# Chunk outputs with swapped operands and TensorE transposes, and a zero fill moved to another place on ScalarE, in a two-block transformer kernel

## Chip, cores, metric

The kernel runs on one core of one Trainium2 chip. The metric is device time in microseconds (us) of one execution. A core has five engines with a program each: TensorE (PE, with its weight loads PEld), VectorE (DVE), ScalarE (ACT), GpSimd (POOL) and SyncE (SP). Each works off its own instructions in order; semaphores hold one back until what it needs is there. Sixteen DMA engines move data between DRAM and the on-chip memory; SP and ACT issue the transfers that matter here, and a row "SPq" or "ACTq" is the stretch in which an engine issues one.

## What is computed

Two blocks on a sequence of 256 tokens of width 1024 in float32. The change touches the first half of the first block only:

```
x = concat(meta_tokens[16], x[256])            # 272 positions
p = rms_norm(x) @ w_in                          # q 512, k 128, v 128, u 512
a = sliding_window_attention(q, k, v)           # 8 heads of 64, window 128, sinks, meta keys always seen
s = s5_ssm(u)                                   # 32 groups of 16 channels, 64 complex states each
    bu = u B;  state[t] = A * state[t-1] + bu[t];  y = Re(C state) + D u
    z  = gelu(y);  s = z * sigmoid(z @ glu_w + glu_b)
h = x + concat(rms_norm(a), rms_norm(s)) @ w_out
```

After it come a product-key expert layer (PEER: 16384 experts, 8 heads with 16 experts each per token, with a weighted scatter and two large matrix products) and a second block of two attention layers. They are the remaining 1200 us, and neither the code nor the order of their instructions changes.

## The kernel before

**Matrix products.** Large products split each float32 operand into a rounded part and a rest and run three matmuls (`mm3`, lines L1696 to L1698). Weights come through a feed `w` (L89, issued on SP); ACT rounds each (`H`, L102) and DVE or POOL makes the rest (`Lo`, L103).

**The SSM in chunks.** Time is cut into 34 chunks of 8 steps. `Ssm.enter` puts u through DRAM (`udr`, L552) and loads it as `U` (L556: 128 rows of step and channel, 32 groups, 34 chunks). `powers` builds maps `W` on DVE; `maps` transposes them on PE (L566) and ACT copies them to `WT` (L567). `outputs` builds tables `G` on DVE (L595 to L600, two tensors of 2304 columns). In `run`, 32 matmuls of `U` with `WT` (L639; the trace has two instructions for each) give the state inputs, which ACT copies (`s`, L644); DVE rotates, scans and rotates back to the chunk states `S` (L652 to L671). `response` multiplies `bd` and `G` on PE (L613) to the impulse response `K`, which goes to DRAM (`kdr`, L621) and comes back as the block matrix `T` (L625). A chunk output is `T` times `U` (L684) plus `G` times `S` (L691), four pairs of groups into each of four PSUM banks, taken in turn from tags y (one bank), b (two banks), y and b; ACT applies the Gelu (`zc`, L694); 16 stores and 4 loads through DRAM (`zdr`, L698; `zT`, L700) turn it to channels by time. `zT` is multiplied by the gating weights `glu` (L712), then come tanh (L736), the product `z` (L738) and the rounded `zH` (L739), the input of the SSM half of the output product.

**The attention.** The q product (L1696 to L1698 into p), its norm and transposes (L333), scores (L369), exps (L378), then for each of two token halves: transposes of the weights (L397), ACT copies (`PT`, L399), products with the values (L406, L410), `attn` (L414), norm and transposes (L423), `aH` (L424), and the attention half of the output product (`out_part`).

**What sets the order.** The attention part is written as the foreground, the SSM part as a background generator that is given room in nanoseconds by its `yield` numbers. A scheduler takes instructions in about that order, and explicit `c.after(a, b)` puts a behind b.

**The zero fill.** Expert weights are later scattered into a DRAM table `wscr` of 8 MB that must hold zeros. A tile `zero` of 128 by 256 is cleared on POOL, and four ACT-issued transfers of 2 MB each (L256) write it, behind the last `hH` turn (L233).

Of the kernel before, what the change touches and what calls it, by code (L numbers as in the profile page):

```python
# [19 lines left out]
FT = mybir.dt.float32  # L20
# [3 lines left out]
AF = mybir.ActivationFunctionType  # L24
# [149 lines left out]
SJ = 8  # L174
SC = L // SJ


def first_half(c):

    nc, tc, A = c.nc, c.tc, c.A  # L180
    V, G = nc.vector, nc.gpsimd
    f = Flow(c)
    with ExitStack() as ctx:
        one = ctx.enter_context(tc.tile_pool(name="b1", bufs=1, reuse_waits="tile"))
        pin = tc.tile_pool(name="b1in", bufs=1, side="right", reuse_waits="tile")
        inp = pin.__enter__()
# [9 lines left out]
        pk = one.tile([128, NPK1], FT, name="pk1")  # L196
        nc.sync.dma_start(pk, A["pk1"])
        c.feed.load(4)
        zero = inp.tile([128, 256], FT, name="zero")
        c.memset0 = G.memset(zero, 0.0)  # L200

        def P1(n):
            if n in PKA:
# [48 lines left out]
        ssm.enter(up)  # L252
        ssm.tables()
        ssm.outputs()
        for i in range(4):
            z = nc.scalar.dma_start(c.wscr[:, 32 * i:32 * i + 32].rearrange("p b t -> p (b t)").rearrange("p (a n) -> p a n", n=256),  # L256
                                    zero[:, None, :].to_broadcast([128, 16, 256]))
            c.after(z, c.turned)


        vr = one.tile([128, 2, 128], FT, name="vr")
# [4 lines left out]
        glu = None  # L266
# [86 lines left out]
        def attention():  # L353
# [4 lines left out]
            with tc.tile_pool(name="b1a", bufs=1, side="right", reuse_waits="tile") as work:  # L358
# [3 lines left out]
                for th in range(2):  # L362
# [19 lines left out]
                    nc.scalar.copy(Pm, S[:, :, 0:16])  # L382
                    ready.append((S, st, Pm))
                f.mark("exps")
                for th in range(2):
                    S, st, Pm = ready[th]
                    jobs = [(Pm.rearrange("p h m -> p (h m)"), None)]
                    jobs += [(S[:, h, 16 + 128 * kb:144 + 128 * kb], (h, kb)) for h in range(8) for kb in range(th + 1)]
                    o = c.psum("o")
                    prev = None  # L390
                    for j0 in list(range(0, len(jobs), 4)) + [None]:
                        nxt = None
                        if j0 is not None:
                            p = c.psum("m")
                            grp = jobs[j0:j0 + 4]
                            for n, (ap, _) in enumerate(grp):
                                nc.tensor.transpose(p[:, n * 128:(n + 1) * 128], ap, c.ident)  # L397
                            PT = work.tile([128, 512], FT, tag="PT", name="PT", bufs=2)
                            nc.scalar.copy(PT[:, :len(grp) * 128], p[:, :len(grp) * 128])  # L399
                            nxt = (grp, PT)  # L400
                            yield 109 * len(grp)
                        if prev:
                            for n, (_, hk) in enumerate(prev[0]):
                                lhs = prev[1][:, n * 128:(n + 1) * 128]
                                if hk is None:
                                    nc.tensor.matmul(o, lhs, vb.rearrange("p k r d -> p r k d"), start=True, stop=True)  # L406
                                    continue
                                h, kb = hk
                                b = 64 * (h % 2)
# [28 lines left out]
class Ssm:  # L438
# [3 lines left out]
    def __init__(self, c, one, P1):  # L442
        self.c, self.nc, self.one, self.P1 = c, c.nc, one, P1
        self.V = c.nc.vector

    def temp(self, name, i):
        return self.one.tile([128, 2304], FT, tag="t%d" % i, name=name)
# [180 lines left out]
    def run(self, glu, out):  # L628
        nc, c, V, one = self.nc, self.c, self.V, self.one
        yield 8000  # L630
        self.maps()
        yield 3000

        st = self.temp("s", 0)[:, :2 * 16 * SC].rearrange("p (z j c) -> p z j c", z=2, j=16)
        for j0, n in ((0, 6), (6, 5), (11, 5)):
            for z in range(2):
                p = c.psum("b")
                for j in range(j0, j0 + n):
                    nc.tensor.matmul(p[:, (j - j0) * 2 * SC:(j - j0 + 1) * 2 * SC], self.WT[z][:, j],  # L639
                                     self.U[:, 2 * j:2 * j + 2].rearrange("p g c -> p (g c)"), start=True, stop=True)  # L640
                v = p[:, :n * 2 * SC].rearrange("p (j g c) -> p j g c", j=n, g=2)
                for g in range(2):
                    r = slice(64 * g, 64 * g + 64)
                    nc.scalar.copy(st[r, z, j0:j0 + n], v[r, :, g])  # L644
            yield 500
        self.response()

        flat = lambda t: t.rearrange("p j c -> p (j c)")
        both = lambda z: self.R[:, None, z].to_broadcast([128, 2, 16, SC])
# [21 lines left out]
                V.tensor_tensor(S[z][r, :, g], m1[r, z, :, 1:SC - 1], m2[r, 1 - z, :, 1:SC - 1], op=(OP.subtract, OP.add)[z])  # L671
        yield 2000

        zc = self.temp("zc", 3)[:, :32 * (SC - 2)].rearrange("p (g c) -> p g c", g=32)
        self.zT = self.temp("zT", 0)[:, :4 * T].rearrange("p (a t) -> p a t", a=4)
        n = SC - 2
        dst = c.zdr.rearrange("(g p) i c -> p i g c", p=16)
        for ct in range(4):
            y = c.psum("yb"[ct % 2])
            for jj in range(4):  # L680
                j = 4 * ct + jj
                for g in range(2):
                    o = 2 * jj + g
                    m = nc.tensor.matmul(y[:, o * n:(o + 1) * n], self.T[:, 2 * j + g], self.U[:, 2 * j + g, 2:],  # L684
                                         start=(o == 0), stop=False, skip_group_check=True)
                    if o == 0:
                        first = m
                    else:
                        c.after(m, first)
                for z in range(2):  # L690
                    nc.tensor.matmul(y[:, 2 * jj * n:2 * (jj + 1) * n], self.G[z][:, j, 1:].rearrange("p a b -> p (a b)"),  # L691
                                     S[z][:, j].rearrange("p g c -> p (g c)"), start=False, stop=(z == 1), skip_group_check=True)
            gs = slice(8 * ct, 8 * ct + 8)
            nc.scalar.activation(zc[:, gs].rearrange("p g c -> p (g c)"), y[:, :8 * n], AF.Gelu)  # L694
            if ct % 2:
                h = slice(8 * ct - 8, 8 * ct + 8)
                for i in range(SJ):
                    nc.sync.dma_start(dst[:, i, h], zc[16 * i:16 * i + 16, h])  # L698
                for k in (ct - 1, ct):
                    t = nc.sync.dma_start(self.zT[:, k], c.zdr[k * 128:(k + 1) * 128].rearrange("p i c -> p (i c)"))  # L700
            yield 1500
        self.had.append(t)
        yield "exps"
        acc = [c.psum("b") for _ in range(2)]
        yield 8000

        for u, i in [(10, 0)] + [(u, 1) for u in range(11, 15)] + [(u, 2) for u in range(15, 19)]:
            if u < len(c.feed.issued):
                c.after(c.feed.issued[u], self.had[i])
        for k in range(4):  # L710
            for co in range(4):
                m = nc.tensor.matmul(acc[co // 2][:, co % 2 * T:co % 2 * T + T], glu()[:, k * 512 + co * 128:k * 512 + (co + 1) * 128], self.zT[:, k],  # L712
                                     start=(k == 0 and co % 2 == 0), stop=(k == 3), skip_group_check=True)
                if k == 0:
                    if co % 2:
                        c.after(m, first)
                    first = m
            yield 500
# [918 lines left out]
def body(tc, A, out):  # L1637
# [3 lines left out]
    with ExitStack() as ctx:  # L1641
# [79 lines left out]
        c.hscr = hscr = tc.dram_tile([128, 2, D], FT, name="hscr")  # L1721
        c.udr = tc.dram_tile([512, SJ, SC], FT, name="udr")
        c.kdr = tc.dram_tile([512, (2 * SJ - 1) * 16], FT, name="kdr")
        c.zdr = tc.dram_tile([512, SJ, SC - 2], FT, name="zdr")
        c.ascr = [tc.dram_tile([128, AB, T], FT, name="ascr%d" % i) for i in range(NB // AB)]
        c.wscr = tc.dram_tile([128, NB, 128], FT, name="wscr")
        with tc.tile_pool(name="ph", bufs=1, reuse_waits="tile") as ph:
# [51 lines left out]
def layout(inp):  # L1779
# [15 lines left out]
    A["wkv"] = chunks(w[:, 512:768])  # L1795
    A["wu"] = chunks(w[:, 768:])
    wo = g["w_out"][0]
    wo = np.concatenate([wo[:512][qp], wo[512:]], 0)
    A["wo"] = np.concatenate([chunks(wo[r:r + 512, n:n + 512]) for r in (0, 512) for n in (0, 512)], 1)
    A["glu"] = chunks(g["ssm_glu_w"][0])  # L1800

    def states(a):
        return a.reshape(16, 128).T
# [4 lines left out]
    def col(v, k):  # L1808
        return v.reshape(k, 128).T
# [4 lines left out]
    for p in range(16):  # L1814
# [6 lines left out]
          dk, col(g["ssm_glu_b"][0], 4), col(g["attn_out_g"][0][qp], 4), col(g["ssm_out_g"][0], 4),  # L1821
# [69 lines left out]
```

## Time and profile before

| | us |
|---|---|
| median of 3 runs | 1386.55 (1384.66 to 1387.51) |
| profiled execution | 1384.22, span 1382.4 |
| PE busy | 1290.8 (93%) |
| DVE, ACT, POOL busy | 931.5 (67%), 646.9 (47%), 419.9 (30%) |
| mean granted TensorE clock | 0.953 |

Times within the trace count from the start of the span. The part that the change touches ends with the first `zH` matmul, at 184.02 us; from there on the instructions of PE, DVE, ACT and SP stand in the same order before and after the change. A granted clock of 1.00 is the higher of TensorE's two levels, 0.50 the lower.

### The profile page before, as it was taken

How to read it: one execution, taken by the hardware profiler on the slowest of the kernel's cores; microseconds unless marked ns; L12 is line 12 of the kernel's file. 1: busy time of each engine (PE TensorE's matmuls, PEld its weight loads, DVE VectorE, ACT ScalarE, POOL GpSimd, SP SyncE). 2: the span in 40 equal slices, each digit the busy share in tenths (PEclk: the TensorE clock that was granted, in tenths of full speed). 3: DMA queues.
4: the chain of work that ended last, by engine and by line, in shares of the span. 5: the costliest groups of instructions: out<-in, count | busy, mean ns of one | idle time of the engine just before them, and what ended most of it. 6: DMA issues, size and time to landing. Idle time of an engine off the chain costs nothing.

```text
span 1382.4 us, 21238 instructions
## 1 busy us (share of the span) xinstructions
PE 1290.8 (93%) x7800; PEld 1121.0 (81%) x7800; DVE 931.5 (67%) x2135; ACT 646.9 (47%) x1119; POOL 419.9 (30%) x253
## 2 busy tenths in 40 slices
PE   4678999999999999998999999999998979979998
PEld 4555989999999999998777788888866768756777
DVE  6963278898898666664888855555567855585734
ACT  4324245545545444444444454444554545534552
POOL 7000000377787777700000000000033426441143
PEclk9876699999999999999999999999999999997999
DMA  5927166688887777897889866555564325551231
GB/s 198 305 36 132 24 225 209 205 218 227 228 225 212 200 204 194 241 367 241 302 300 317 298 201 193 185 191 188 187 207 140 107 95 171 202 161 53 77 107 61
DMA packets 118392, 263.80 MB, mean 191 GB/s; under 512 B 35968, under 2 KB 50176, under 8 KB 117008
## 3 DMA queue, kind: packets, MB, share of 16 engines
q1 hardware_dynamic: 80208, 228.82, 52.6%
q0 software_dynamic: 20608, 8.46, 5.2%
q10 hardware_dynamic: 17472, 25.17, 5.0%
q8 instruction: 61, 1.00, 0.3%
q14 instruction: 43, 0.35, 0.1%
HBM read 233.24 MB, written 28.90 MB: 190 GB/s over the span
## 4 chain that ended last, share of the span: by engine, by line
PE 77%; DVE 13%; DMA 6%; ACT 2%; issue 2%; SPq 0%; ACTq 0%; DVEq 0%
PE ps L884 20%; PE ps L1696 10%; PE ps L1697 10%; PE ps L1698 10%; PE pr L1696 4%; PE pr L1698 4%; PE pr L1697 4%; DMA ga<-ascr 3%; PE m L1289 2%; DVE Lo L103 2%; PE ps L1097 2%; PE o L1334 1%; DMA wscr<-zero 1%; DVE act L894 1%; PE m L369 1%
## 5 line engine op out<-in xcount | busy, mean ns | idle before, releaser
L102 ACT CAST H<-w 128x1024 fp32r<-128x1024 f32 (+1 forms) x370 | 385.9, 1045 | 513.0 <-PE ps L1697 186.1
L103 DVE TENSOR_TENSOR Lo<-w,H 128x1024 fp32r<-128x1024 f32 x310 | 387.5, 1251 | 183.3 <-ACT H L102 179.8
L103 POOL TENSOR_TENSOR Lo<-w,H 128x1024 fp32r<-128x1024 f32 (+1 forms) x60 | 142.1, 2373 | 629.1 <-ACT H L102 604.2
L1055 POOL DMA_INDIRECT wscr<-sent x128 | 241.2, 1884 | 234.2 <-DVE act L1032 169.0
L1696 PE MATMUL ps<-xH,H 128*128 128x256 f32 x1024 | 290.9, 284 | 0.0
L1697 PE MATMUL ps<-xL,H 128*128 128x256 f32 x1024 | 287.9, 281 | 0.0
L1698 PE MATMUL ps<-xH,Lo 128*128 128x256 f32 x1024 | 287.7, 281 | 0.0
L884 PE MATMUL ps<-H,a 128*128 128x512 f32 x1024 | 281.5, 397 | 5.0 <-ACT a L896 3.0
L884 PEld LDWEIGHTS ps<-H,a 128*128 128x128 f32 x1024 | 193.8, 189 | 51.0 <-ACT a L896 3.2
L1696 PEld LDWEIGHTS ps<-xH,H 128*128 128x128 f32 x1024 | 193.1, 189 | 0.0
L1698 PEld LDWEIGHTS ps<-xH,Lo 128*128 128x128 f32 x1024 | 193.1, 189 | 0.0
L1697 PEld LDWEIGHTS ps<-xL,H 128*128 128x128 f32 x1024 | 193.0, 188 | 0.0
L884 PE MATMUL ps<-Lo,a 128*128 128x512 f32 x512 | 161.5, 397 | 1.4 <-DVE Lo L103 1.3
L884 PEld LDWEIGHTS ps<-Lo,a 128*128 128x128 f32 x512 | 96.5, 189 | 25.4 <-DVE Lo L103 3.2
L894 DVE TENSOR_TENSOR act<-ga,act 128x256 f32<-128x256 f32 x128 | 47.4, 420 | 27.4 <-DMA ga<-ascr 27.3
L1696 PE MATMUL pr<-H,exH 128*128 128x512 f32 x128 | 54.7, 429 | 0.9 <-ACT exH L1137 0.9
L1696 PE MATMUL pr<-H,oxH 128*128 128x512 f32 (+1 forms) x128 | 52.8, 415 | 1.1 <-ACT oxH L1137 1.1
L897 DVE TENSOR_TENSOR a<-act,a 128x256 fp32r<-128x256 f32 x128 | 53.5, 419 | 0.0
L1697 PE MATMUL pr<-Lo,exH 128*128 128x512 f32 x128 | 52.8, 413 | 0.0
L896 ACT CAST a<-act 128x256 fp32r<-128x256 f32 x128 | 51.3, 401 | 2.9 <-DVE act L894 2.9
L1698 PE MATMUL pr<-H,exL 128*128 128x512 f32 x128 | 52.6, 411 | 0.0
L1698 PE MATMUL pr<-H,oxL 128*128 128x512 f32 (+1 forms) x128 | 52.6, 411 | 0.0
(486 smaller groups left out, 1975.1 us busy)
## 6 DMA issues: line engine op xcount, KB each, us to landing
w<-in_ut SPq DMA_DIRECT2D x128, 512.0 KB
w<-in_pv SPq DMA_DIRECT2D x128, 512.0 KB
ascr<-ga ACTq DMA_DIRECT2D x64, 256.0 KB
ga<-ascr SPq DMA_DIRECT2D x64, 256.0 KB
w<-in_we SPq DMA_DIRECT2D x32, 512.0 KB
w<-in_wod SPq DMA_DIRECT2D x28, 512.0 KB
wscr<-zero ACTq DMA_DIRECT2D x4, 2048.0 KB
w<-in_wqy SPq DMA_DIRECT2D x16, 512.0 KB
```

What stands on the lines that cost most here:

```text
L102: self.last = self.nc.scalar.copy(H, self.loaded[u])
L103: eng.tensor_sub(Lo, self.loaded[u], H.bitcast(FT))
L884: nc.tensor.matmul(acc[2 * th + n], a[:, s], b[:, n * 512:(n + 1) * 512], start=first and e == 0, stop=last and e == 2)
L894: V.tensor_tensor(src, ga[:, blk % 2], src, op=OP.mult)
L896: copied = nc.scalar.copy(aH, src)
L897: V.tensor_sub(aL, src, aH.bitcast(FT))
L1055: ins = c.nc.gpsimd.indirect_dma_start(out=c.wscr.rearrange("i b (t o) -> (i b t) o", o=1), out_offset=bass.IndirectOffsetOnAxis(ap=t.bitc ...
L1097: nc.tensor.matmul(p[:, a * 128:(a + 1) * 128], o1[:, a], o2[:, a], start=True, stop=True)
L1289: nc.tensor.matmul(sp[:, :off + nk], q(h)[:, ts], k(h)[:, :off + nk], start=True, stop=True)
L1696: nc.tensor.matmul(o, ah, bh, start=first, stop=False)
L1697: nc.tensor.matmul(o, ah, bl, start=False, stop=False)
L1698: nc.tensor.matmul(o, al, bh, start=False, stop=last)
```

## The change

1. The zero fill is issued on ACT behind the first Gelu of the chunk outputs instead of behind the last `hH` turn; its source is 128 by 128 (`self.zero`), so that each store covers 512 bytes in place of 1024.
2. `response()` comes right behind `maps()`, ahead of the state matmuls.
3. In the chunk outputs `U` (32 columns, at column position 0 or 32) and `S` (64 columns) are the stationary operands, `T` and `G` the moving ones, so that results have chunks on 64 partitions; 16 PE transposes (L704) and two DVE copies (L705) make `zT` in place of the 16 stores and 4 loads. The rows of the affected weights are permuted on the host (`cp`) to suit.
4. The transposes of the attention weights stand behind the last chunk output (`c.weighed`), a `yield` falls from 8000 to 1500, and four output weight loads no longer stand behind `zT`.

```diff
-        zero = inp.tile([128, 256], FT, name="zero")
-        c.memset0 = G.memset(zero, 0.0)
...
-        for i in range(4):
-            z = nc.scalar.dma_start(c.wscr[:, 32 * i:32 * i + 32].rearrange("p b t -> p (b t)").rearrange("p (a n) -> p a n", n=256),
-                                    zero[:, None, :].to_broadcast([128, 16, 256]))
-            c.after(z, c.turned)
...
-                                nc.tensor.transpose(p[:, n * 128:(n + 1) * 128], ap, c.ident)
+                                c.weighed.append(nc.tensor.transpose(p[:, n * 128:(n + 1) * 128], ap, c.ident))
...
         self.maps()
+        self.response()
         yield 3000
...
-        self.response()
...
-                    m = nc.tensor.matmul(y[:, o * n:(o + 1) * n], self.T[:, 2 * j + g], self.U[:, 2 * j + g, 2:],
-                                         start=(o == 0), stop=False, skip_group_check=True)
...
+                    m = nc.tensor.matmul(y[q:q + 32, o], self.U[:, 2 * j + g, 2:], self.T[:, 2 * j + g], start=(jj == 0), stop=False,
+                                         tile_position=(0, q), skip_group_check=True)
...
-                    nc.tensor.matmul(y[:, 2 * jj * n:2 * (jj + 1) * n], self.G[z][:, j, 1:].rearrange("p a b -> p (a b)"),
-                                     S[z][:, j].rearrange("p g c -> p (g c)"), start=False, stop=(z == 1), skip_group_check=True)
...
+                    m = nc.tensor.matmul(y[0:64, o], S[z][:, j].rearrange("p g c -> p (g c)"), self.G[z][:, j, 1:].rearrange("p a b -> p (a b)"),
+                                         start=False, stop=(z == 1), skip_group_check=True)
...
+            t = nc.scalar.activation(zc[0:64, h, :, j0:j0 + 4].rearrange("p i j q -> p j i q"),
+                                     y[0:64].rearrange("p (j i q) -> p j i q", j=4, i=SJ), AF.Gelu)
+            if b == 0:
+                for i in range(4):
+                    m = nc.scalar.dma_start(c.wscr[:, 32 * i:32 * i + 32].rearrange("p b t -> p (b t)").rearrange("p (a n) -> p a n", n=128),
+                                            self.zero[:, None, :].to_broadcast([128, 32, 128]))
+                    c.after(m, t)
...
-                for i in range(SJ):
-                    nc.sync.dma_start(dst[:, i, h], zc[16 * i:16 * i + 16, h])
-                for k in (ct - 1, ct):
-                    t = nc.sync.dma_start(self.zT[:, k], c.zdr[k * 128:(k + 1) * 128].rearrange("p i c -> p (i c)"))
...
+        for h in range(2):
+            p = c.psum("by"[h])
+            for i in range(SJ):
+                nc.tensor.transpose(p[:, 64 * i:64 * i + 64], zc[0:64, h, i].rearrange("p j q -> p (j q)"), c.ident[:64, :64])
+            V.tensor_copy(self.zT[:, 2 * h:2 * h + 2].rearrange("p g (i c) -> p g i c", i=SJ), p.rearrange("p (i g c) -> p g i c", i=SJ, g=2))
...
+        for m in c.weighed:
+            c.after(m, self.ylast)
```

On ACT, around the zero fill before (L233 the turn, L536 and L551 copies for the SSM, L102 the rounding of weights, L286 the first step of the k norm):

```order
L233 ACTIVATE hH<-m,pka 128x272 x2
L256 DMA wscr<-zero 128x16x256
L102 CAST H<-w 128x1024
L536 COPY bd_401<-pre 64x16x16 x2
L536 COPY bd_402<-pre 64x16x16 x2
L551 COPY uP<-p 128x34x8 x2
L551 COPY uP<-y 128x34x8
L551 COPY uP<-o 128x34x8
L256 DMA wscr<-zero 128x16x256 x3
L102 CAST H<-w 128x1024 x2
L286 ACTIVATE ks<-p 128x128
```

On ACT, around the zero fill after the change (L372 are the exps, L693 the Gelus, L394 the copies of the transposed attention weights):

```order
L372 ACTIVATE S,st<-S,st 128x272 x7
L376 COPY Pm<-S 128x128
L102 CAST H<-w 128x1024 x2
L693 ACT_TABLE_LOAD
L693 ACTIVATE zc<-y 64x4x8x16
L697 DMA wscr<-zero 128x32x128 x4
L693 ACTIVATE zc<-b 64x4x8x16
L693 ACTIVATE zc<-y 64x4x8x16
L693 ACTIVATE zc<-b 64x4x8x16
L394 COPY PT<-m 128x512 x2
L394 COPY PT<-m 128x128
```

All four transfers now stand together between the first and the second Gelu, ahead of every copy of attention weights.

On PE before, where the chunk outputs begin (L1696 to L1698 are the attention half of the output product):

```order
L1696 MATMUL p<-H,aH 128x512
L1697 MATMUL p<-Lo,aH 128x512
L1698 MATMUL p<-H,aL 128x512
L684 MATMUL y<-U,T 128x32 x2
L691 MATMUL y<-S,G_479 128x64
L691 MATMUL y<-S,G_480 128x64
L684 MATMUL y<-U,T 128x32 x2
```

On PE after the change, from the last chunk output pair to the products with the values (L392 transposes of attention weights, L704 those of `zc`, L717 the gating product, L405 products with the values):

```order
L683 MATMUL b<-T,U 32x128 x2
L689 MATMUL b<-G_478,S 64x128
L689 MATMUL b<-G_479,S 64x128
L392 MATMUL m<-cstt,Pm 128x128
L392 MATMUL m<-cstt,S 128x128 x7
L704 MATMUL b<-cstt,zc 128x64 x8
L704 MATMUL y<-cstt,zc 128x64 x8
L401 MATMUL o<-vb,PT 128x512
L405 MATMUL o<-vr,PT 128x64 x3
L392 MATMUL m<-cstt,S 128x128
L405 MATMUL o<-vr,PT 128x64 x4
L717 MATMUL b<-zT,glu 128x256 x4
```

The chunk outputs moved from inside the attention half of the output product to between scores and weighing, and the gating product from behind that half to inside the weighing.

On DVE, the tables `G` before (L103 is the rest of a weight, L287 and L1706 begin the norm of k):

```order
L595 TENSOR_TENSOR G_479<-pk_107,A 128x2304
L598 TENSOR_TENSOR G_480<-pk_107,A 128x2304
L607 MEMSET K 128x4x112
L103 TENSOR_TENSOR Lo<-w,H 128x1024 x2
L287 TENSOR_REDUCE kss<-ks 128x2 x2
L287 TENSOR_REDUCE kss<-ks 16x2
L103 TENSOR_TENSOR Lo<-w,H 128x1024
L1706 TENSOR_SCALAR rs<-kss 128x6
```

The same place after the change (L281 begins the norm of k):

```order
L592 TENSOR_TENSOR G_478<-pk_106,A 128x2304
L592 TENSOR_TENSOR tg<-pk_106,A 128x2304
L595 TENSOR_TENSOR G_479<-pk_106,A 128x2304
L594 TENSOR_TENSOR G_478<-G_478,tg 128x2304
L596 TENSOR_TENSOR tg<-pk_106,A 128x2304
L103 TENSOR_TENSOR Lo<-w,H 128x1024
L597 SCALAR_TENSOR_TENSOR G_479<-G_479,tg 128x2304
L103 TENSOR_TENSOR Lo<-w,H 128x1024
L281 TENSOR_REDUCE kss<-ks 128x2 x2
L281 TENSOR_REDUCE kss<-ks 16x2
```

The six table operations now stand nearly together; before, two stood ahead of the k norm and four were placed among its steps.

## Rows read from the trace of the kernel before

**Rows 1.** Chain that ended last, 115 to 190 us: start us, us, what

```profile
124.81 0.48 ACT PT L399
...
136.70 0.70 DVE attn L414
...
138.56 0.50 PE p L1696
...
143.63 0.36 PE y L684 x4
...
165.50 0.53 PE p L1696
...
176.21 6.06 PE b L712 x28
182.29 0.48 ACT tg L736
...
184.02 0.50 PE p L1696
```

**Rows 2.** The same view, 24 to 126 us

```profile
39.65 18.49 DMA wscr<-zero
58.16 7.69 DMA U<-udr
...
65.98 10.05 PE b L639 x46
...
86.44 1.97 PE b L639 x18
...
89.07 1.29 DVE m L652
```

**Rows 3.** Timeline of ACT, 30 to 60 us

```profile
33.78 0.39 ACTq L256 DMA_DIRECT2D wscr<-zero  x1
...
38.31 1.24 ACTq L256 DMA_DIRECT2D wscr<-zero  x1
...
39.65 12.87 ACTq L256 DMA_DIRECT2D wscr<-zero  x2
52.62 1.99 ACT L102 CAST H<-w 128x1024 fp32r<-128x1024 f32 x2 [12.21 <-issue]
```

**Rows 4.** DMA queues, 33 to 52.52 us: packets, MB, share of 16 engines

```profile
q10 hardware_dynamic: 5065, 5.15, 76.3%
```

**Rows 5.** DMA queues, 52.52 to 70 us

```profile
q10 hardware_dynamic: 3191, 3.23, 52.1%
```

**Rows 6.** Timeline of PE, 45 to 100 us

```profile
65.98 10.05 PE L639 MATMUL b<-U,WT 128*128 128x68 f32 x46 [3.88 <-DMA U<-udr]
...
89.77 2.03 PE L613 MATMUL m<-G,bd 128*32 128x128 f32 x64
```

**Rows 7.** Timeline of DVE, 36 to 95 us

```profile
51.08 2.55 DVE L595 TENSOR_TENSOR G<-pk,A 128x2304 f32<-128x2304 f32 x1
...
59.28 1.20 DVE L103 TENSOR_TENSOR Lo<-w,H 128x1024 fp32r<-128x1024 f32 x1
...
69.74 2.56 DVE L600 SCALAR_TENSOR_TENSOR G<-G,tg 128x2304 f32<-128x2304 f32 x1
```

**Rows 8.** Windows of core 0: busy us by engine, granted TensorE clock (PEclk), DMA share

```profile
66.00:76.00 10.00, 10.00 (x47) 10.00 (x48) 7.05 (x8) 2.23 (x8) 0.00 (x0) 0.50 0.01 3
86.00:88.00 2.00, 2.00 (x18) 1.91 (x18) 0.00 (x0) 0.59 (x2) 0.00 (x0) 1.00 0.00 0
```

**Rows 9.** Timeline of ACT, 118 to 190 us

```profile
142.90 1.28 ACT L694 ACT_TABLE_LOAD   x1
147.19 0.38 ACT L694 ACTIVATE zc<-y 128x256 f32<-128x256 f32 x1 [3.00 <-PE y L691]
```

**Rows 10.** DMA queues, 48 to 58 us

```profile
q10 hardware_dynamic: 3197, 3.24, 94.4%
q1 hardware_dynamic: 1758, 0.23, 15.2%
```

More of the change, by code (lines that the diff above doesn't have):

```diff
@@ L384, in attention @@
                 f.mark("exps")
+                c.weighed = []
                 for th in range(2):
@@ L444, in __init__ @@
         self.V = c.nc.vector
+        self.zero = one.tile([128, 128], FT, name="zero")
+        c.nc.gpsimd.memset(self.zero, 0.0)
     def temp(self, name, i):
@@ L644, in run @@
                     nc.scalar.copy(st[r, z, j0:j0 + n], v[r, :, g])
-            yield 500
-        self.response()
+            yield 0
         flat = lambda t: t.rearrange("p j c -> p (j c)")
@@ L672, in run @@
         yield 2000
-        zc = self.temp("zc", 3)[:, :32 * (SC - 2)].rearrange("p (g c) -> p g c", g=32)
+        zc = self.temp("zc", 3)[:, :2048].rearrange("p (h i j q) -> p h i j q", h=2, i=SJ, j=8)
         self.zT = self.temp("zT", 0)[:, :4 * T].rearrange("p (a t) -> p a t", a=4)
         n = SC - 2
-        dst = c.zdr.rearrange("(g p) i c -> p i g c", p=16)
-        for ct in range(4):
-            y = c.psum("yb"[ct % 2])
+        for b in range(4):
+            y = c.psum("yb"[b % 2])
+            prev = None
@@ L680, in run @@
             for jj in range(4):
-                j = 4 * ct + jj
+                j = 4 * b + jj
+                o = slice(128 * jj, 128 * jj + 128)
                 for g in range(2):
-                    o = 2 * jj + g
-                    m = nc.tensor.matmul(y[:, o * n:(o + 1) * n], self.T[:, 2 * j + g], self.U[:, 2 * j + g, 2:],
-                                         start=(o == 0), stop=False, skip_group_check=True)
[L686 to L689, printed above, removed]
@@ L690, in run @@
-                for z in range(2):
-                    nc.tensor.matmul(y[:, 2 * jj * n:2 * (jj + 1) * n], self.G[z][:, j, 1:].rearrange("p a b -> p (a b)"),
-                                     S[z][:, j].rearrange("p g c -> p (g c)"), start=False, stop=(z == 1), skip_group_check=True)
[L693 to L696, printed above, removed]
-                for i in range(SJ):
-                    nc.sync.dma_start(dst[:, i, h], zc[16 * i:16 * i + 16, h])
-                for k in (ct - 1, ct):
-                    t = nc.sync.dma_start(self.zT[:, k], c.zdr[k * 128:(k + 1) * 128].rearrange("p i c -> p (i c)"))
@@ L701, in run @@
-            yield 1500
-        self.had.append(t)
+                    q = 32 * g
+                    m = nc.tensor.matmul(y[q:q + 32, o], self.U[:, 2 * j + g, 2:], self.T[:, 2 * j + g], start=(jj == 0), stop=False,
+                                         tile_position=(0, q), skip_group_check=True)
+                    if prev is not None:
+                        c.after(m, prev)
+                    prev = m
+                for z in range(2):
+                    m = nc.tensor.matmul(y[0:64, o], S[z][:, j].rearrange("p g c -> p (g c)"), self.G[z][:, j, 1:].rearrange("p a b -> p (a b)"),
+                                         start=False, stop=(z == 1), skip_group_check=True)
@@ new lines, in run @@
+            self.ylast = m
+            h, j0 = b // 2, 4 * (b % 2)
+            t = nc.scalar.activation(zc[0:64, h, :, j0:j0 + 4].rearrange("p i j q -> p j i q"),
[5 more added lines that the diff above has]
+                    c.after(m, t)
@@ L703, in run @@
+            yield 500
+        for h in range(2):
[3 more added lines that the diff above has]
+            V.tensor_copy(self.zT[:, 2 * h:2 * h + 2].rearrange("p g (i c) -> p g i c", i=SJ), p.rearrange("p (i g c) -> p g i c", i=SJ, g=2))
         yield "exps"
         acc = [c.psum("b") for _ in range(2)]
-        yield 8000
-        for u, i in [(10, 0)] + [(u, 1) for u in range(11, 15)] + [(u, 2) for u in range(15, 19)]:
+        yield 1500
@@ L708, in run @@
+        for u, i in [(10, 0)] + [(u, 1) for u in range(11, 15)]:
             if u < len(c.feed.issued):
                 c.after(c.feed.issued[u], self.had[i])
+        for m in c.weighed:
+            c.after(m, self.ylast)
         for k in range(4):
@@ L1723, in body @@
         c.kdr = tc.dram_tile([512, (2 * SJ - 1) * 16], FT, name="kdr")
-        c.zdr = tc.dram_tile([512, SJ, SC - 2], FT, name="zdr")
         c.ascr = [tc.dram_tile([128, AB, T], FT, name="ascr%d" % i) for i in range(NB // AB)]
@@ L1797, in layout @@
     wo = g["w_out"][0]
-    wo = np.concatenate([wo[:512][qp], wo[512:]], 0)
+    cp = np.arange(512).reshape(2, 8, 2, 16).transpose(0, 2, 1, 3).reshape(-1)
+    wo = np.concatenate([wo[:512][qp], wo[512:][cp]], 0)
     A["wo"] = np.concatenate([chunks(wo[r:r + 512, n:n + 512]) for r in (0, 512) for n in (0, 512)], 1)
-    A["glu"] = chunks(g["ssm_glu_w"][0])
+    A["glu"] = chunks(g["ssm_glu_w"][0][cp][:, cp])
     def states(a):
@@ L1820, in layout @@
           g["ssm_c_im"][0].transpose(0, 2, 1).reshape(16, 128, 16).transpose(1, 0, 2).reshape(128, 256),
-          dk, col(g["ssm_glu_b"][0], 4), col(g["attn_out_g"][0][qp], 4), col(g["ssm_out_g"][0], 4),
+          dk, col(g["ssm_glu_b"][0][cp], 4), col(g["attn_out_g"][0][qp], 4), col(g["ssm_out_g"][0][cp], 4),
           np.tile(g["q_norm_g"][0], 2)[:, None], np.tile(g["k_norm_g"][0], 2)[:, None], rep(g["attn_sinks"][0][QPERM])]
```

## The prediction

> **What bounds the kernel now.** The kernel is one long chain that runs mostly through PE, so I read first the part of the chain of waits that the change touches. What begins with the first zH matmul at 184.02 us [rows 1] keeps its order, so the whole effect should be by how much that matmul moves. In the front, the chain runs through the zero fill and the loads of U behind it until 65.85, then through the state matmuls, the DVE chain from 89.07 on and the attention [rows 2]. At the back it is PE almost without a gap: weighing, the start of the output product at 138.56, chunk outputs from 143.63 to 165.50, the rest of the output product, the gating product to 182.27 [rows 1].
>
> The second view is the timeline of ACT around the zero fill. Four transfers of 2048 packets of 1 KB each are issued there. The first two take 0.39 and 1.24 us, the last two 12.87 us together, and the next instruction of ACT waited 12.21 us for "issue", for nothing else [rows 3]. The queue tells why: by the end of the issue, at 52.52, 5065 packets had moved [rows 4], and 3191 (a few seen in both stretches) moved afterwards [rows 5]. So ACT is let go when no more than about 3100 packets are left in its queue; until then it does nothing.
>
> **The front.** Without the fill, U's loads needn't share the DMA engines with it, and ACT isn't held from 39.65 to 52.52. This removes PE's wait of 3.88 us for U at 65.98 [rows 6]. But response() now stands ahead of the state matmuls and needs both finished tables G. DVE is packed: the first table operation starts at 51.08, behind the maps W, whose place doesn't move [rows 7]. Six of them at 2.55 us and one weight rest of 1.20 [rows 7] make 51.1 + 15.3 + 1.2 = 67.6, less a little overlap 67.5 (tables finished at 72.30 before, when nothing was in a hurry). PE then starts at 67.5 instead of 65.98. It runs the response in 2.03 us at the higher clock [rows 6], twice that at the lower, and then state matmuls. The 64 of these took 10.05 + 1.97 us before, 0.218 us each in the first stretch and 0.109 in the second [rows 2], at a granted clock of 0.50 and 1.00 [rows 8], half and full clock in the following. If the short response raises the clock earlier, up to 4 us come back. Sum: +1.5 for the start, +2.0 to +4.1 for the response (before, it lay at 89.77, under the DVE chain, and cost nothing there), +0.7 for three more q rows ahead of the last state matmul, 0 to -4 for the clock: from 0 to +6. Since q's sums are worked into the same chain later than the start of it, a part is absorbed; I take **+1.7**, with -1 to +4 as its ends. The scores keep their length, so the exps end at 124.81 + 1.7 = 126.5.
>
> **The zero fill in its new place.** It now stands on ACT behind the first Gelu. From 126.5, ACT does two casts (1.99 for two, [rows 3]), the table load (1.28, [rows 9]) and a Gelu of 64x512 (0.38 for 128x256 [rows 9], so 0.4 to 0.76): the issue starts at 130.5. There are now 4 x 4096 = 16384 packets of 512 bytes. ACT comes free when some 3100 are left, after 13284. A packet's cost: in one stretch 3197 packets of 1 KB took 94.4% of 16 engines for 10 us, 47.2 ns each, and 1758 of 131 bytes took 15.2%, 13.8 ns each [rows 10]. A line through both gives 27.9 ns at 512 bytes, over 16 engines 1.74 ns; by bytes alone it would be 23.6 (1.48 ns), by count alone 47 (2.95 ns). So 13284 packets take 23.2 us, from 19.6 to 39; I take the line, and expect small packets to be near its end. Before, packets moved at 2.95 ns each only after the first 2 to 3 us; add 1.5 to 2. That gives a release between 152 and 156, with the two weight loads that share the engines perhaps 158; I take **154.5**.
>
> Queued behind on ACT are three Gelus and all copies of attention weights (PT). The products with the values wait for PT, the transposes of zc for the Gelus, the gating product for those. PE has only the chunk outputs to do meanwhile, and the first eight transposes of attention weights. Those 128 chunk instructions now stream 128 columns. Bounds: 0.032 us each as in the response, which puts four 32-column tiles beside one another [rows 6], 0.11 to 0.22 as the state matmuls: 4 to 28 us from 121.3 on. Even 28 ends at 149, inside the hold. So swapping the operands neither gains nor costs: it is hidden, and with it the 21.9 us that the chunk outputs took before (143.63 to 165.50, [rows 1]) leave the path, to be replaced by the hold.
>
> **From the release to zH.** Three Gelus, 2.0. The rest of the transposes of zc ahead of the first value product, about 8 at 0.11 to 0.22, +1. From the first PT copy to the start of the output product 13.75 us as before (124.81 to 138.56, [rows 1]). Inside it now the gating product, 6.06 us for 28 of 32 instructions [rows 1], 6.9 in all, of which about 1 fits into PE's waits: +6. The output product, contiguous, 48 matmuls at 0.23 (10.71 us for 165.50 to 176.21 with 30 of them, partly at half clock [rows 1]): 11.6. Its tail: before, the additions into h ran under the gating product, and tanh, z and zH took 182.29 to 184.02, 1.73 [rows 1]. Now tanh is early, but two additions of 128x512 (about 0.7 each, as attn in [rows 1]) and z stand behind the last matmul: 3. Sum 2 + 1 + 13.75 + 6 + 11.6 + 3 = 37.35. So zH's first matmul starts at 154.5 + 37.35 = 191.9, against 184.02: **+7.9 us**. The bounce through DRAM is gone, but the chain did not hold it: in between PE had chunk outputs and output product to do [rows 1].
>
> **Against a rule.** The row shows ACT held for 12.21 us by issue alone [rows 3]. The Trainium skill, in "DMA: Bandwidth & Descriptors", section "Issuing engines are not separate DMA queues", says that starting transfers takes a sequencer a time that is usually small beside the transfer. By that, ACT would go on at about 131 and the first rival below would come true; the trace disagrees for a fill this large, and I go by the trace.
>
> **Rivals.**
> (a) *Faster: ACT isn't held long.* The first two issues of 0.39 and 1.24 us [rows 3] speak for it, the other two against. The queue would have to take the four transfers by bytes or by number. Then PE's chunk outputs set the time from 121.3: 14 us (full clock) and 37.35 less the Gelus' 2 reach zH at 171, 28 us (half clock) at 185. That is -13 to +1, in the middle -6: 1380 on the scale of the medians. It decides if the hold, with its start, is under 184.02 - 37.35 - 130.5 = 16 us.
> (b) *No change.* The hold is near 16 us, because 512 bytes go at the rate of bytes and more remains in the queue (one and a half transfers, 6100 packets: 10280 x 1.48 = 15.2): 1386.5.
> (c) *Much slower.* Packets cost nearer to 47 ns, by count: release at 171, zH at 209: 1411. Only a part of that way is likely: the row of 131 bytes speaks against it [rows 10].
> (d) *The swap itself is slow.* Alternating between tiles of 32 and 64 columns, each of 32 switches empties the array. At half clock 28 us + 32 x 0.22 = 35 from 121.3: 156, the release I forecast; it adds 1.5 at most to my sum, but turns (a) into +8 on its own. No row of before alternates.
> The Trainium skill, in "TensorEngine Tiling (Array Packing)", section "Key Properties", says that a change of tiling mode drains TensorE, which speaks for (d); no run here shows it yet.
>
> **How the numbers follow.** The profiled execution took 1384.22, the median is 1386.55, 2.3 more. 1384.2 + 7.9 = 1392.1 in the one, 1394.5 in the other. A measurement can tell about 0.2% (2.8 us) from no change. Chances: the forecast 0.50, (c) and (d) beyond it 0.10, (b) 0.15, (a) 0.25. The likeliest case's own range is 1389 to 1400 (release 149 to 160). To leave out no more than 2 in 10 the range reaches into (a), to 1378, and up to 1402. Faster 0.25, same 0.15, slower 0.60.
>
> **What would show it.** In the profile after: ACT with a gap of 20 to 25 us on "issue" between the first and the second Gelu (a gap under 16 proves me wrong); PE idle before the first value product, with ACT as releaser; packets of the ACT queue at 25 to 31 ns; state matmuls free of their wait for U but response waiting for G at 67 to 68; exps ending at 125 to 131; zH 36 to 40 us behind the release; the chunk outputs' end ahead of the release. Wrong would be: a second ACT Gelu right behind the first, or chunk outputs that end last.

## The result, and the profile after

The changed kernel takes 1394.44 us (median of 7 runs, 1391.66 to 1397.39) against 1386.58: ratio 1.0058, 95% interval 1.0043 to 1.0073. It is 7.9 us slower, and 1394.5 was forecast. The total is right; of the steps that led to it several are wrong, and their errors cancel. That the two totals agree to 0.1 us is luck. The trace shows the steps first.

The front. Timeline of PE after the change (start us, us, instruction, in brackets the wait before it and what ended it):

```profile
60.42 0.60 PE L610 MATMUL m<-G,bd 128*32 128x128 f32 x2 [7.02 <-DVE G L594]
66.40 3.32 PE L610 MATMUL m<-G,bd 128*32 128x128 f32 x62 [5.38 <-DVE G L597]
69.65 4.24 PE L637 MATMUL b<-U,WT 128*128 128x68 f32 x36
```

Response waits for the tables G, as forecast, until 66.4 (67.5 forecast). But the 36 state matmuls behind it take 0.116 us each, full clock, where before 46 took 0.218 [rows 2]. The DVE chain starts at 84.66 instead of 89.07, the exps end at 120.67 instead of 124.81. The start of that chain on DVE, and the last piece of the exps on ACT:

```profile
84.66 1.29 DVE L649 TENSOR_TENSOR m<-s,R 128x1088 f32<-128x1088 f32 x1 [2.20 <-ACT s L642]
```
```profile
120.48 0.19 ACT L372 ACTIVATION_READ_ACCUMULATOR S<-S,st 128x1 f32 x1
```

The hold. Timeline of ACT after the change:

```profile
121.34 7.12 ACTq L697 DMA_DIRECT2D wscr<-zero  x2
121.85 1.04 ACT L102 CAST H<-w 128x1024 fp32r<-128x1024 f32 x1
122.91 1.28 ACT L693 ACT_TABLE_LOAD   x1
124.21 0.59 ACT L693 ACTIVATE zc<-y 64x512 f32<-64x512 f32 x1
128.50 15.00 ACTq L697 DMA_DIRECT2D wscr<-zero  x2
143.55 0.59 ACT L693 ACTIVATE zc<-b 64x512 f32<-64x512 f32 x1 [18.75 <-issue]
```

Four issues in a row, and a second Gelu 18.75 us behind the end of the first, with nothing to wait for but issue: the row of before with 12.21 [rows 3], longer. (A row marked x2 is two issues, one behind the other.) The first issue starts at 121.34, ahead of a cast, the table load and the Gelu that stand before it in ACT's program: it depends on none of them, and is taken while they still run. Of the DMA queues, 143.5 to 160 us, and 132 to 140 us (packets, MB, share of 16 engines):

```profile
q10 hardware_dynamic: 5455, 2.78, 58.2%
```
```profile
q10 hardware_dynamic: 5306, 2.70, 112.4%
```

ACT is let go with some 5400 packets left (a few are seen on both sides of the cut), not 3100. In the second stretch the packets take 112.4% x 16 x 8 us / 5306 = 27 ns each (27.9 forecast); a share above 100% means that packets overlap on an engine.

What waits for it. Waits of PE, 110 to 200 us (total, times, longest):

```profile
PE b L704 <- ACT zc L693: 10.8, 1, 10.8
PE p L1701 <- ACT zH L744: 3.5, 1, 3.5
```

Chunk outputs end at 132.4; behind them PE does eight transposes of weights, then stands still 10.8 us for the Gelu, and once more 3.5 us for zH. The chain after the change, 30 to 200 us:

```profile
124.80 3.70 issue
128.50 8.81 ACTq L697
137.35 6.15 ACTq L697
143.55 0.60 ACT zc L693
...
146.27 2.00 PE o L401 x2
...
168.23 0.80 PE p L1701
...
184.56 0.54 DVE z L743
185.12 0.52 ACT zH L744
185.68 0.79 PE p L1701
```

The fill is on the chain itself now, as "issue" and ACTq. But the first zH matmul starts at 185.68, only 1.66 us later than before [rows 1]. Where is the rest? Windows of core 0 (busy us by engine, granted clock, DMA share, GB/s), before and after:

```profile
184.00:194.00 10.00, 9.98 (x51) 8.48 (x52) 8.06 (x27) 4.23 (x7) 0.00 (x0) 1.00 0.27 87
```
```profile
134.00:144.00 10.00, 0.00 (x0) 0.00 (x0) 0.00 (x0) 0.45 (x1) 0.00 (x0) 0.68 1.07 319
184.00:194.00 10.00, 8.32 (x26) 7.06 (x27) 5.35 (x13) 2.95 (x8) 0.00 (x0) 0.56 0.26 82
```

Behind zH the clock is at its lower level after the change and at its higher before: from 185.3 to 198.9 us the same matmuls take 0.43 us in place of 0.23. The store of h that ends the first half, in the timeline of SP before and after:

```profile
198.22 0.33 SPq L1733 DMA_DIRECT2D hscr<-h  x1
```
```profile
205.95 0.33 SPq L1737 DMA_DIRECT2D hscr<-h  x1
```

It comes 7.7 us later: 1.7 until zH and 6 behind it. From there on the two traces run side by side, most of the way 6.5 to 8.5 us apart until 1120 us. A longer half-clock stretch there, 17.1 us against 6.8, adds some 4 more, so that the two profiled executions end 11.9 us apart, where the medians differ by 7.9.

Each kernel was profiled in one execution, and places in a trace vary. In the eight kernels below and above that have the same code up to there, the first operation on the tables G starts between 48.9 and 51.6 us. So single places are good to one or two us, and the parting into 1.7 and 6 holds for this pair of traces.

### The profile page after: what moved, and what is told of

The parts are those of the page before. It is cut to its first block, busy times and chain, and to the rows that moved or that the text cites. A ratio compares the mean times of both kernels' runs of the same rounds, so it can differ in the third digit from the quotient of the medians.

```text
span 1394.3 us, 21243 instructions
## 1 busy us (share of the span) xinstructions
PE 1292.2 (93%) x7816; PEld 1112.2 (80%) x7816; DVE 931.9 (67%) x2137; ACT 648.2 (46%) x1119; POOL 424.1 (30%) x253
## 4 chain that ended last, share of the span: by engine, by line
PE 79%; DVE 13%; issue 2%; ACT 2%; DMA 2%; ACTq 1%; SPq 0%; DVEq 0%
PE ps L889 24%; PE ps L1701 10%; PE ps L1702 10%; PE ps L1703 9%; PE pr L1701 4%; PE pr L1703 4%; PE pr L1702 4%; PE m L1294 3%; PE ps L1102 2%; DVE Lo L103 2%; PE o L1339 1%; ACTq L697 1%; DVE rs L1718 1%; DMA ga<-ascr 1%; PE m L363 1%
## 5 line engine op out<-in xcount | busy, mean ns | idle before, releaser
L102 ACT CAST H<-w 128x1024 fp32r<-128x1024 f32 (+1 forms) x370 | 385.9, 1044 | 505.1 <-PE ps L1702 193.2
L103 DVE TENSOR_TENSOR Lo<-w,H 128x1024 fp32r<-128x1024 f32 x310 | 386.3, 1247 | 178.9 <-ACT H L102 175.4
L103 POOL TENSOR_TENSOR Lo<-w,H 128x1024 fp32r<-128x1024 f32 (+1 forms) x60 | 141.8, 2367 | 626.5 <-ACT H L102 613.0
L1060 POOL DMA_INDIRECT wscr<-sent x128 | 246.0, 1922 | 246.1 <-DVE act L1037 181.1
```

Of the source, the lines that this page charges most:

```text
L102: self.last = self.nc.scalar.copy(H, self.loaded[u])
L103: eng.tensor_sub(Lo, self.loaded[u], H.bitcast(FT))
L1060: ins = c.nc.gpsimd.indirect_dma_start(out=c.wscr.rearrange("i b (t o) -> (i b t) o", o=1), out_offset=bass.IndirectOffsetOnAxis(ap=t.bitc ...
```

## The experiments

Each was timed in five rounds against the kernel before (1385.7 to 1386.3 in those rounds).

**1. The fill on SP.** From the changed kernel:

```diff
-                    m = nc.scalar.dma_start(c.wscr[:, 32 * i:32 * i + 32]...
+                    m = nc.sync.dma_start(c.wscr[:, 32 * i:32 * i + 32]...
```

> The changed kernel with the four fill transfers issued by SP instead of ACT, behind the same Gelu; nothing else. Theory of the hold (ACT can do nothing from 121.3 to 143.5 us because its own queue is full): the Gelus follow at once, PE loses its wait of 10.8 us, the first zH matmul comes at 174 to 176 instead of 185.7, and the time falls to 1380 to 1385; to 1376 if the half-clock stretch behind zH (13.7 us) goes too. Rival (it is the fill's traffic that costs, or weight loads that now queue behind it on SP): the time stays within 3 us of 1394.4.

Measured: 1375.21, ratio 0.9915 (0.9899 to 0.9930), faster than both. SP issued it earlier than I had said (104.5 to 127.2 us), since the `after` sets an order and no wait: the issue runs ahead of the first Gelu at 125.03. Timeline of ACT:

```profile
125.03 0.59 ACT L693 ACTIVATE zc<-y 64x512 f32<-64x512 f32 x1
126.00 0.59 ACT L693 ACTIVATE zc<-b 64x512 f32<-64x512 f32 x1 [0.37 <-PE b L689]
129.69 0.59 ACT L693 ACTIVATE zc<-y 64x512 f32<-64x512 f32 x1 [3.10 <-PE y L689]
133.38 0.59 ACT L693 ACTIVATE zc<-b 64x512 f32<-64x512 f32 x1 [3.10 <-PE b L689]
```

The Gelus now wait for PE, not PE for them. PE's only long wait left is the 3.5 us for zH; its first matmul starts at 169.46, and half clock follows from 169.4 to 183.0. My forecast of 1380 to 1385 with zH at 174 to 176 missed: zH came 5 us sooner still. Windows of core 0:

```profile
134.00:144.00 10.00, 10.00 (x66) 8.20 (x66) 2.07 (x3) 3.13 (x7) 0.00 (x0) 1.00 0.56 178
...
170.00:180.00 10.00, 10.00 (x33) 8.49 (x32) 3.79 (x12) 2.62 (x5) 0.00 (x0) 0.50 0.11 43
```

The hold costs 19 us of the median: 16.2 until zH, the rest behind it, where the profiles can't be told from run-to-run variation. Of the 16.2, 10.8 are PE's wait. Most of the rest is clock: with the hold PE works at half clock from 144.2 to 154.6 and from 168.2 to 171.6, and without it the clock is full from 121.6 to 169.4. I estimate 7 us for that, half of these 13.8 us. The two come to a little more than 16.2, as the front of that trace is 0.9 us later (scores at 103.3).

The rival of traffic falls. The same 16384 packets move, though earlier than in the changed kernel. In the second kernel of experiment 5, where SP issues the fill later, they move beside the Gelus, and no Gelu is held and PE waits for none. Its rows on SP and ACT, and its window:

```profile
119.39 28.87 SPq L697 DMA_DIRECT2D wscr<-zero  x4
```
```profile
132.43 0.59 ACT L693 ACTIVATE zc<-b 64x512 f32<-64x512 f32 x1 [2.66 <-PE b L689]
```
```profile
134.00:144.00 10.00, 10.00 (x84) 6.91 (x82) 0.00 (x0) 2.52 (x5) 0.00 (x0) 1.00 1.06 312
```

**2. The fill in its old place and size.** From the changed kernel, the four issues back on ACT behind the last hH turn, with 1 KB packets:

```diff
+        for i in range(4):
+            z = nc.scalar.dma_start(c.wscr[:, 32 * i:32 * i + 32]..., ssm.zero[:, None, :].to_broadcast([128, 16, 256]))
+            c.after(z, c.turned)
...
-            if b == 0:
-                for i in range(4):
-                    m = nc.scalar.dma_start(...)
```

> The changed kernel with the fill in its old place and size (ACT, behind the last hH turn, 1 KB packets). Theory of the hold: the late hold goes (10 to 11 us), the early one comes back and delays casts, WT copies and U again: exps end 3 to 5 us later than at 120.9. Together 1386 to 1390 with the half-clock stretch behind zH, 1380 to 1384 without. Rival (swapped chunk outputs or the order of attention weighing cost the time): 1394 or more.

Measured: 1374.84, ratio 0.9917 (0.9903 to 0.9931); scores begin at 104.3 (102.4 in the changed kernel). Lower than I had expected: against experiment 1 the early hold costs nothing in the median. The 2 us at the scores are not clear of variation (101.1 to 104.1 in the other traces of the changed front), and the half-clock stretch behind zH was 6.8 us long here, 13.6 there, behind the same wait of 3.5 us. So the change without the fill's new place and size is a gain of 11 us, and the two together are a loss of 19 to 20. Experiment 3 parts them: about 10 us are the place, at 1 KB packets and with what it does to the front, and 9 the halved packets in that place.

**3. 1 KB packets in the new place.**

```diff
-        self.zero = one.tile([128, 128], FT, name="zero")
+        self.zero = one.tile([128, 256], FT, name="zero")
```

(and the views of the four transfers to suit)

> The changed kernel with 1 KB packets in the fill (source 128x256 as before the change), still on ACT in the new place. If a packet costs 27 ns at 512 bytes and 46 ns at 1 KB, and ACT is let go with about 3100 packets left, the hold ends after 5100 packets of 2.9 ns, 15 us, 6 to 7 us earlier than at 143.5: zH near 179, 1387 to 1389. If it is let go with a fixed number of bytes or transfers left (5400 packets of 512 bytes were left, 1.3 transfers), it ends after 5500 packets, 16 us: 1388 to 1390. Rival (the size of packets is nothing to the hold): 1394.

Measured: 1385.29, ratio 0.9989 (0.9975 to 1.0003), 9 us under the changed kernel, and a little under both forecasts (1387 to 1390). The issue lasts from 123.2 to 140.6, 17.4 us in place of 22.2; PE's wait for the Gelu is 6.1 in place of 10.8, zH comes at 180.36, and the stretch at half clock is 10.2 us long in place of 13.6. DMA queues, 140.63 to 160 us:

```profile
q10 hardware_dynamic: 3517, 3.57, 54.1%
```

**4. The fill in 16 transfers.** From the changed kernel, 16 issues of 1024 packets of 512 bytes each:

```diff
-                for i in range(4):
+                for i in range(16):
```

> The changed kernel with the fill cut into 16 transfers of 1024 packets of 512 bytes, on ACT in the same place. When ACT was let go, 5423 of 16384 packets (1.3 of 4 transfers) had not started. If the queue holds a number of transfers, only about 1300 to 1400 packets are left at the end, the hold is 4000 packets x 1.69 ns = 7 us longer, and the time is 1398 to 1402. If it holds a number of packets, the hold ends as before, 1393 to 1396.

Measured: 1397.39, ratio 1.0090 (1.0068 to 1.0113). PE's wait for the Gelu grew to 16.7 us, the issue to 28.1 (120.0 to 148.1). DMA queues, 148.09 to 160 us:

```profile
q10 hardware_dynamic: 2404, 1.21, 34.4%
```

The time lies between my two forecasts, and neither of my two rules holds alone. With what is left in four cases less one whole transfer: 2404 - 1024 = 1380; 5455 - 4096 = 1359; 3517 - 2048 = 1469; before, 3191 - 2048 = 1143 [rows 5]. So an issue ends when the last transfer is accepted, which happens with some 1100 to 1500 packets of those ahead of it still to go. The median rose by 3 only of the 6 us that the hold grew, though zH came 5.1 later in the trace. The six executions spread from 1394.7 to 1402.0, so how much of the 6 reaches the median isn't settled.

**5. response() back behind the state matmuls**, once in the changed kernel and once in the one with the fill on SP:

```diff
         self.maps()
-        self.response()
         yield 3000
...
-            yield 0
+            yield 500
+        self.response()
```

> The changed kernel with response() back behind the state matmuls. If its move paid in the front (exps end at 120.9 us now, 124.8 before the change), exps come 2 to 4 us later, and hold and rest shift with them: 1396 to 1398. Rival (the front became faster because the fill left it, and the move was nothing or cost something): exps end at 117 to 121, 1391 to 1394.

> The kernel with the fill on SP, and response() back behind the state matmuls. With the fill on ACT that put the scores 3.2 us later (105.6 instead of 102.4). If the move of response is worth this, scores begin at 106 and the time is 1377 to 1379. Rival (it only shifted against the hold, or a later T holds the chunk outputs back): within 1 us of 1375.2.

Measured: 1392.50, ratio 1.0051 (1.0031 to 1.0071), with scores at 105.6 in place of 102.4; and on SP 1379.89, ratio 0.9947 (0.9928 to 0.9966), with scores at 107.4 in place of 103.3. The move makes the front 3 to 4 us shorter: with response at its old place PE waits 16.3 us for `ks`, a step of the k norm on DVE, and with the move it does the response in part of that time (waits of 7.0 and 5.4 us). In the median the move is worth 4 to 5 without the hold, a little more than I had expected. Two things stand behind that number beside the front. PE waits 1.8 us for T. And the twelve executions spread: three took under 1375 us, at a mean granted clock of 0.962, the other nine over 1377, at 0.954 to 0.959. With the hold the later scores cost nothing in the median: my expectation of 1396 to 1398 missed, zH was 3 us later, but the half-clock stretch behind it 6.8 us long in place of 13.6.

**6. Matmuls in the gap before zH.** Eight products that nobody reads are added between the two halves of the output product, in the changed kernel and in the one with the fill on SP:

```diff
+        warm = c.psum("b")
+        for i in range(8):
+            nc.tensor.matmul(warm[:, :T], glu[:, i * 128:(i + 1) * 128], ssm.zT[:, i % 4], start=True, stop=True)
         work = ctx.enter_context(tc.tile_pool(name="b1g", bufs=1, side="right", reuse_waits="tile"))
```

> The changed kernel with eight more matmuls (parts of glu times zT into a free bank, 0.43 us each at full clock, never read) between the attention half and the SSM half of the output product, where PE stands 3.7 us before zH. Theory of the clock (PE's wait of 3.7 us before zH is why the granted clock falls to 0.50 from 185.3 to 198.9, which costs 6 us): no half-clock stretch behind zH, 1387 to 1390. Rival (the clock falls whatever PE does there, or falls from the work before it): the stretch stays and the time is 1394 or a little more.

> The kernel with the fill on SP (1375.2 us, half clock from 169.4 to 183.0) and the same eight matmuls ahead of zH. Theory of the clock: no half-clock stretch behind zH, 1367 to 1371. Rival: 1375 to 1376.

Measured: 1389.54, ratio 1.0030 (1.0013 to 1.0047), and 1373.50, ratio 0.9901 (0.9883 to 0.9920). The added work delays zH, to 191.74 from 185.68 in the first, and still the median is 5 us lower. The trace shows less: its store of h comes at 204.52, 1.4 us sooner than in the changed kernel, and where the rest comes from isn't known. Windows of core 0, first kernel:

```profile
184.00:194.00 10.00, 8.77 (x40) 7.53 (x41) 6.89 (x19) 3.85 (x9) 0.00 (x0) 0.83 0.33 103
194.00:204.00 10.00, 10.00 (x47) 8.09 (x46) 7.73 (x20) 3.48 (x4) 0.00 (x0) 1.00 0.34 105
```

The half-clock stretch shrinks from 13.6 to 3.4 us (186.5 to 189.9), and lies mostly on the added matmuls. They started late (they wait 1.87 us for their bank), so PE was still idle for a while; on SP the gain was 1.7, not clear of the noise and less than the 4 that I had expected at least, since zH came 4.8 us later (174.30).

**7. No gap at all.** On top of the fill on SP, tanh, z, zH and zL are computed right behind the gating product (the code of `ssm_glu` cut in two, its tensors in freed buffers):

```diff
-        out["glu"] = acc
+        out["z"] = ssm_glu(c, self.one, self.temp, pool(), self.P1, self.zT, acc)
...
-        zH, zL, zr = ssm_glu(c, work, P1, ssm.zT, res["glu"])
+        zH, zL, sqs = res["z"]
+        zr = ssm_rs(c, gpool, sqs)
```

> The kernel with the fill on SP, and tanh, z, zH and zL computed right behind the gating product, ahead of the second half of the attention's weighing, instead of behind the attention half of the output product; no work is added or left out. PE then needn't wait between the two halves (3.9 us), and by the theory of the clock the half-clock stretch (6 us) goes too: 1365 to 1369. If DVE and ACT, which now do this inside the weighing, delay the second attn by 2 to 4 us: 1368 to 1371. Rival of the clock (it falls anyway): 1371 to 1374.

Measured: 1368.63, ratio 0.9869 (0.9850 to 0.9889), the fastest here. The second attn is 2.8 us later (154.5), the wait for zH is gone. Timeline of PE (`gzr` is zH), and windows:

```profile
169.96 0.39 PE L1712 MATMUL p<-H,aL 128*128 128x512 f32 x1
170.72 0.47 PE L1710 MATMUL p<-H,gzr 128*128 128x512 f32 x1 [0.38 <-DVE h L344]
```
```profile
160.00:170.00 10.00, 9.74 (x43) 7.55 (x41) 6.75 (x17) 3.33 (x4) 0.00 (x0) 1.00 0.34 105
170.00:180.00 10.00, 9.62 (x42) 7.52 (x41) 6.24 (x7) 3.72 (x4) 0.00 (x0) 1.00 0.53 161
180.00:190.00 10.00, 8.90 (x66) 7.97 (x65) 8.54 (x20) 7.59 (x15) 0.00 (x0) 1.00 0.81 270
```

zH's first matmul is 1.3 us later than with the fill on SP alone, yet the kernel is 6.6 us faster: behind zH the clock stays at its higher level. A stretch of 3.4 us at half clock now lies inside the weighing (156.5 to 159.9). The edit also moves work of ACT and DVE, so that it shows what closing the gap is worth as a whole, and not the clock's part alone.

**8. The kernel before with the fill on SP**, behind the loads of T:

```diff
-        for i in range(4):
-            z = nc.scalar.dma_start(c.wscr...)
-            c.after(z, c.turned)
...
         self.had.append(t)
+        for i in range(4):
+            z = nc.sync.dma_start(c.wscr..., self.zero[:, None, :].to_broadcast([128, 32, 128]))
+            c.after(z, t)
```

> The kernel before the change with the fill alone moved: on SP behind the loads of T, 512-byte packets, chunk outputs and all the rest as before. If the removal of the early fill is what made the front faster, scores start at 102 to 104 instead of 106.6 and the time is 1381 to 1384. If response's move did that (with response at its old place scores began at 105.6), it is 1384 to 1387. Against 1375.2 with the fill on SP in the changed kernel, the difference is what chunk outputs, transposes and the new order are worth.

Measured: 1386.96, ratio 1.0010 (0.9998 to 1.0023); scores at 106.1. The 18.5 us of fill in the chain of before [rows 2] were worth nothing. The trace says why. The state matmuls start at 52.78, 13 us earlier, but without the early fill the scheduler places all six table operations ahead of the k norm, and PE then waits for DVE. Waits of PE, 48 to 92 us:

```profile
PE p L1696 <- DVE ks L285: 16.3, 1, 16.3
```

So the experiment tests the fill's removal together with this new order on DVE, which the changed kernel has too.

**9. Swapped operands and transposes in the old order.** From the kernel with the fill on SP:

```diff
-        yield 1500
+        yield 8000
...
-        for m in c.weighed:
-            c.after(m, self.ylast)
```

> The kernel with the fill on SP, swapped operands and TensorE transposes, but with the weighing not tied behind the chunk outputs and the old yield of 8000: PE then does weighing, part of the output product, chunk outputs, transposes, gating product, as before the change. If the swap with its transposes is the gain of 11 us over the kernel before, 1375 to 1378. If the order is the gain (chunk outputs while ACT does the exps, gating product inside the weighing), 1384 to 1387. Half and half, 1379 to 1382, if the shorter chunk outputs (16.5 us in place of 21.8) are all that the swap gives.

Measured: 1384.85, ratio 0.9992 (0.9976 to 1.0007). The chunk outputs take 14.8 us (141.1 to 155.9), zH comes at 176.09, 8 us earlier than before the change; then PE has waited 2.8 us for zH, the clock is at half from 177.7 to 187.9, and most of it is lost again. So the order that the change sets is worth 10 of the 11 us. Swap, transposes and the earlier response together show 2 us in the old order (against experiment 8), which the two intervals can't tell from nothing; in the trace the half clock behind zH takes back most of what they gain until there. The swap by itself wasn't run.

## Why the prediction was right, and where its steps were not

**The cause was right.** A fill on ACT in the middle of the attention holds ACT by issue, PE waits for the Gelu behind it, and the chunk outputs are hidden by that. Experiment 1 takes the hold away with everything else in place, and the kernel becomes faster than before; experiment 2 does the same in another way. Rival (a), that ACT isn't held long, fell with the row of 18.75 us; its time, 1380, is about what the change gives without the hold (1375).

**The first step that failed: "the whole effect should be by how much that matmul moves".** zH's first matmul moved by 1.66 us, not 7.9. The other 6 us arose behind it, where instructions and their order are the same: at half clock. PE waited 3.5 us for zH after the change and 0.9 before. Filling the gap shortens the stretch (6), removing it takes it away (7). But the wait doesn't set the length: behind the same 3.5 us the half clock lasted 13.6 us here and in experiment 1, 10.2 in experiment 3 and 6.8 in experiment 2. What share of the effect is the gap itself and what share the work ahead of it isn't settled.

**The front: the sign was wrong, +1.7 forecast, -4.1 measured.** I knew that the clock could give back up to 4 us and counted on part of it only; all state matmuls behind the short response ran at full clock, and so did the k and q products between them. With response back at its old place the front is 3 to 4 us longer (5), and the fill's removal was worth nothing (8).

**The hold: 154.5 forecast for its end, 143.5 measured.** Of the 11 us, 5.8 are the front. 3.3 are the start: the issue goes ahead of the casts, the table load and the Gelu, which I had added up (130.5). The last 1.8 are its length, 22.2 us in place of 24: a packet cost 27 ns, close to the line; 3100 packets as the rest was wrong, since that is not a constant (4).

**From the release to zH: 37.35 forecast, 42.1 measured.** From the first copy of attention weights to the output product it took 23.2 us where the terms give 20.75, and the output product 14.0 where 11.6 stood (48 x 0.23 is 11.0, a slip in the sum). Both began at half clock (137.5 to 154.6 and 168.2 to 171.6), the first after an idle stretch that I had foreseen without its price. Four of the signs that I had named missed by this and the front: a hold of 18.75 us behind the Gelu (20 to 25), response at 66.4 (67 to 68), exps at 120.67 (125 to 131), and these 42.1 (36 to 40).

So 7.9 us were forecast as a late release; in the traces they came as 1.7 us of release and 6 of clock behind it. Rival (d), tiles of two widths that empty the array, didn't show: a step of two groups takes 0.92 us at full clock after the change (0.41 with U and 0.65 with S stationary, which overlap) and 0.89 before; and the chunk outputs ended at 132.4, 11 us ahead of the release. Timeline of PE after and before:

```profile
122.15 0.41 PE L683 MATMUL b<-T,U 128*32 128x128 f32 x4
122.49 0.65 PE L689 MATMUL b<-G,S 128*64 128x128 f32 x4
```
```profile
146.99 0.58 PE L684 MATMUL b<-U,T 128*128 128x32 f32 x4
147.41 0.64 PE L691 MATMUL b<-S,G 128*128 128x64 f32 x4
```

## What to carry to other kernels

A large transfer issued by a compute engine in many small packets blocks that engine for most of the transfer, here until two thirds of the packets had moved (85% when it was cut in 16); put it on an engine with nothing to do, which here turned a loss of 0.6% into a gain of 0.85%. A stall's price doesn't end with the stall: look at the granted clock of the stretch behind it, and at whether the next wait on PE can be closed by computing its input earlier (another 0.5% here). A transfer that shows as 18 us in the chain can be worth nothing, when PE waits for another engine once it is gone (16.3 us for VectorE here).

## What was not expected of the hardware

An ACT-issued transfer starts while ACT still runs the instructions ahead of it: at 121.34, 3.5 us before the end of the Gelu that stands ahead in its program. And the end of the issue depends on how the transfer is cut: 16384 packets in 4 transfers held ACT's queue for 22.2 us, in 16 transfers for 28.1, with one transfer and some 1400 packets left in both.
